# A two-layer encoder trunk: block products in another order, probability scaling on ScalarE, memory's keys and values first

## The chip, the cores and the metric

The kernel runs on one core of one Trainium2 chip. The metric is device time in microseconds (us) of one execution, the median of several runs; lower is better. The engines of the core have short names in the profile: PE is TensorE (PEld its weight loads), DVE is VectorE, ACT is ScalarE, POOL is GpSimd, and SP is SyncE, which here only issues DMAs. All matrix products are on PE; DVE, ACT and POOL do what lies between them.

## What is computed

The input is x of 512 tokens by 1024, and a memory of 256 tokens by 1024. Two layers follow each other. Each has one wide projection of the normalised x, a token mixer, a cross attention to the memory (4 heads), a SiLU gate and an output projection that is added to x:

```python
h = rmsnorm(x, norm_g[i]);  mem_h = rmsnorm(mem, mem_norm_g[i])
proj = jnp.einsum('bsd,de->bse', h, w_in_a[j])     # layer B: w_in_b
o_mix = mixer_dilated(qkv, ...)                     # layer B: mixer_axial_gqa
o_mem = memory_attention(q_mem, mem_h, w_mem_kv[i], ...)
y = jnp.concatenate([o_mix, o_mem], axis=-1) * jax.nn.silu(gate)
x = x + jnp.einsum('bse,ed->bsd', y, w_out[i])
```

Layer A mixes with three dilated windows per head (8 heads), layer B with grouped-query attention over all 512 tokens (8 query heads). Queries and keys are normalised per head and, in the mixers, rotated; each attention is a softmax over scores.

## The kernel before

**Numbers in two parts.** Every float32 operand of the large products is split into a high part (a cast to fp32r) and a low part (the operand minus the high part). A product is three matmuls: high by high, high by low, low by high (`mm3`, L163 to L165). For weights the high part is `wh`, cast on ACT (`hi`, L282), and the low part `wo`, subtracted on DVE (`lo`, L292); for activations the two parts are made the same way in `split` (L157 on ACT, L160 on DVE).

**Seven block products.** A projection to 512 columns (a chunk) is done as a 2x2 block product with seven products in place of eight. `ORDER` (L173) names the weight blocks in the order of use: the stored blocks "11", "21", "12", "22" and the sums T1, T2, T3, T4 of them. `PRODUCTS` (L347) names the activation block, the PSUM bank (0 or 1) and whether the bank starts afresh: A-blocks "11", "12", "22" and the sums S1, S2, S3, S4. `s_chunk` (L349) runs through them; behind each product an entry of `after` copies the bank to SBUF (`keep`, L357 on ACT) or adds it to what was kept (`add`, L367 on DVE). In the kernel before, the quadrant "22" is a subtraction between two copies in SBUF (L361, DVE), 33 times. The finished quadrant goes on to an `ev` of the chunk (norm, rotation, gate).

**Weights.** The class `Weights` walks through `PLAN`, a list of chunk kinds. It loads tiles of 128x1024 (512 KB) by SP's queue as long as fewer than `KEEP[kind]` tiles are alive. The sum T1 is made on DVE (L251) for chunks ahead of `T1_DMA`, and by an accumulating DMA from POOL's queue for the others; T2, T3 and T4 are accumulating DMAs from POOL's queue always (L256, L261, L266). `KEEP`, `LEAD` and `RING` set how early each is issued.

**The order of the work.** Each engine has its own in-order queue, and the Python code writes them in one pass. `Driver` counts slots, one for each weight tile's products. Side tasks are generators: `urgent` ones (evacuation, norms, preparing the next operand) are stepped when due, `bulk` ones (the attentions) once a slot, with some half-slot steps where `HALF` says so (every third one in two of layer B's gate chunks). A `yield n` puts the next step n slots later, so numbers such as `PD`, `EO`, `Y` and `YB` are waiting times in slots.

**The run through.** Layer A: x is normalised and its rows are transposed into the blocks of H (`put_h`, L461), the first chunk (one set of values, `v0`) starts, and the memory's norm (`mem_norm`) and its keys and values (`mem_kv`, 8 groups of 12 matmuls) come behind it. Then follow the memory's queries, the 8 head chunks with `attn_a` in the background, the three gate chunks (m, a, b), and the output projection. For the latter the gated rows `yf` of the first two gate chunks are the right operand: `prep_y` forms their sums by eight 128x512 subtractions and additions on POOL (L778), then splits each (L759 on ACT, L760 on DVE), while the third gate chunk runs. Then the rest of the projection (`out_rest`), memory's keys and values of layer B, its chunks with `attn_b` (32 steps of a 128-query block) in the background, again three gate chunks with `prep_y`, and the output projection. The rotation table of layer B is made on POOL (L1197, four of 128x512).

**Softmax.** In each attention the reciprocal of the row sum is taken and the probabilities are scaled on DVE: `p` in `attn_a` (L1083, 64 pieces), `pm` in `mem_attn` (L645, 32), `pb` in `attn_b` (L1310, 32). PE transposes the scaled tile next (L1096, L654, L1319). `pipeline` sets the stages of one step: score 0, exponential 1, reciprocal and scale 2, transpose 3, product with the values 4.

## Time and profile before

| what | value |
|---|---|
| time, median of 3 runs (lowest, highest) | 991.82 us (990.87, 992.66) |
| span of the profiled execution | 989.9 us |
| runs above that span | lowest 1.0 us, median 1.9 us |
| mean granted TensorE clock | 0.991 |
| busy: PE, DVE, ACT, POOL | 951.5, 830.3, 644.3, 360.9 us |
| matmuls in the trace | 5724 |
| moved by DMA | 206.13 MB, mean 208 GB/s |

No own time of the profiled execution is listed beside its span: the span goes from the first to the last instruction of the program, and what a run has beyond it is the 1.0 to 1.9 us of the table.

How to read it: PE's busy time is a sum in which neighbouring matmuls overlap, so it is not PE at its peak. But where PE's row is short of the length of a stretch, PE waited. The view of waits lists for each engine what ended each idle time.

### The profile page before, as it was taken

How to read it: one execution, taken by the hardware profiler on the slowest of the kernel's cores; microseconds unless marked ns; L12 is line 12 of the kernel's file. 1: busy time of each engine (PE TensorE's matmuls, PEld its weight loads, DVE VectorE, ACT ScalarE, POOL GpSimd, SP SyncE). 2: the span in 40 equal slices, each digit the busy share in tenths (PEclk: the TensorE clock that was granted, in tenths of full speed). 3: DMA queues.
4: the chain of work that ended last, by engine and by line, in shares of the span. 5: the costliest groups of instructions: out<-in, count | busy, mean ns of one | idle time of the engine just before them, and what ended most of it. 6: DMA issues, size and time to landing. Idle time of an engine off the chain costs nothing.

```text
span 989.9 us, 16669 instructions
## 1 busy us (share of the span) xinstructions
PE 951.5 (96%) x5724; PEld 837.7 (85%) x5724; DVE 830.3 (84%) x1471; ACT 644.3 (65%) x1623; POOL 360.9 (36%) x486
## 2 busy tenths in 40 slices
PE   6999999999999999999999979998999999996998
PEld 4789888888888888888899967887999999985886
DVE  6897788879797979797888998878789998889974
ACT  5656678677777777777775745555677766564750
POOL 2232424565555555555542170124632330115000
PEclk9999999999999999999999989999999999997999
DMA  8989946968777777777769785679685877674532
GB/s 335 309 292 346 225 104 174 295 137 240 182 223 184 221 190 216 189 216 169 237 163 291 173 247 151 254 256 318 173 195 125 241 177 211 179 198 117 160 128 85
DMA packets 86966, 206.13 MB, mean 208 GB/s; under 512 B 25057, under 2 KB 35809, under 8 KB 86882
## 3 DMA queue, kind: packets, MB, share of 16 engines
q1 hardware_dynamic: 70034, 146.28, 42.7%
q0 software_dynamic: 15552, 56.63, 30.3%
q10 hardware_dynamic: 1296, 2.16, 0.6%
q8 instruction: 45, 0.74, 0.3%
q14 instruction: 39, 0.32, 0.1%
HBM read 157.79 MB, written 12.65 MB: 172 GB/s over the span
## 4 chain that ended last, share of the span: by engine, by line
PE 70%; DVE 17%; DMA 7%; issue 3%; ACT 1%; POOL 1%; SPq 1%; DVEq 0%; ACTq 0%; POOLq 0%
PE pj L163 18%; PE pj L165 18%; PE pj L164 18%; DVE wo L292 4%; DMA wl<-in_wall_dram 3%; PE qT L531 2%; DMA og<-od 1%; DVE pb L1310 1%; PE sa L1015 1%; PE pt L1096 1%; DVE sn L367 1%; PE oo L1117 1%; PE sa L1011 1%; PE ptb L1319 1%; PE xT L461 1%
## 5 line engine op out<-in xcount | busy, mean ns | idle before, releaser
L292 DVE TENSOR_TENSOR wo<-wl,wh 128x1024 fp32r<-128x1024 f32 x255 | 315.4, 1243 | 10.1 <-ACT wh L282 9.7
L282 ACT CAST wh<-wl 128x1024 fp32r<-128x1024 f32 x255 | 269.7, 1059 | 73.7 <-PE pj L165 41.2
L163 PE MATMUL pj<-wh,hS 128*128 128x512 f32 (+1 forms) x448 | 164.5, 367 | 0.1
L164 PE MATMUL pj<-wo,hS 128*128 128x512 f32 (+1 forms) x448 | 158.1, 353 | 2.1 <-DVE wo L292 2.0
L165 PE MATMUL pj<-wh,hS 128*128 128x512 f32 (+1 forms) x448 | 158.1, 353 | 0.0
L163 PE MATMUL pj<-wh,h 128*128 128x512 f32 (+1 forms) x336 | 123.2, 367 | 0.8 <-ACT h L157 0.8
L164 PE MATMUL pj<-wo,h 128*128 128x512 f32 (+1 forms) x336 | 118.8, 353 | 1.9 <-DVE wo L292 1.9
L165 PE MATMUL pj<-wh,h 128*128 128x512 f32 (+1 forms) x336 | 118.9, 354 | 0.0
L410 POOL TENSOR_TENSOR rstd<-mse,half 128x4 f32<-128x4 f32 (+2 forms) x98 | 102.0, 1040 | 8.2
L164 PEld LDWEIGHTS pj<-wo,hS 128*128 128x128 f32 x448 | 85.0, 190 | 13.0 <-DVE wo L292 3.2
L165 PEld LDWEIGHTS pj<-wh,hS 128*128 128x128 f32 x448 | 84.7, 189 | 12.2
L163 PEld LDWEIGHTS pj<-wh,hS 128*128 128x128 f32 x448 | 84.8, 189 | 10.2 <-ACT sn L357 0.3
L409 POOL TENSOR_SCALAR mse<-hss 128x4 f32<-128x4 f32 (+1 forms) x86 | 45.3, 526 | 110.5 <-ACT junk L519 103.5
L357 ACT COPY sn<-pj 128x512 f32<-128x512 f32 x132 | 73.5, 590 | 16.5 <-PE pj L165 16.1
L959 POOL TENSOR_TENSOR ta<-sn,tabs 128x128 f32<-128x128 f32 (+1 forms) x64 | 37.0, 580 | 121.1 <-DVE sn L524 81.7
L519 ACT ACTIVATE junk<-sn 128x128 f32<-128x128 f32 x264 | 78.9, 307 | 0.2 <-DVE sn L361 0.2
L164 PEld LDWEIGHTS pj<-wo,h 128*128 128x128 f32 x336 | 64.0, 191 | 9.5 <-DVE wo L292 2.2
L165 PEld LDWEIGHTS pj<-wh,h 128*128 128x128 f32 x336 | 63.7, 190 | 9.2 <-DVE h L160 0.2
L367 DVE TENSOR_TENSOR sn<-pj,sn 128x512 f32<-128x512 f32 x99 | 67.4, 683 | 4.6 <-PE pj L165 4.4
L163 PEld LDWEIGHTS pj<-wh,h 128*128 128x128 f32 x336 | 63.9, 190 | 8.4 <-ACT h L157 1.2
L266 POOL DMA_DIRECT2D wl<-wl x33 | 29.4, 898 | 103.7 <-DVE wo L292 52.3
L163 PE MATMUL pj<-hS,wh 128*128 128x256 f32 x192 | 55.9, 291 | 0.0
(226 smaller groups left out, 2487.1 us busy)
## 6 DMA issues: line engine op xcount, KB each, us to landing
wl<-in_wall_dram SPq DMA_DIRECT2D x222, 512.0 KB, 6.9
wl<-wl POOLq DMA_DIRECT2D x66, 512.0 KB, 5.9
wl<-in_wall_dram POOLq DMA_DIRECT2D x42, 512.0 KB, 8.4
od<-o SPq DMA_DIRECT2D x12, 256.0 KB, 5.0
og<-od SPq DMA_DIRECT2D x12, 256.0 KB, 6.0
odb<-o SPq DMA_DIRECT2D x12, 256.0 KB, 4.0
og<-odb SPq DMA_DIRECT2D x12, 256.0 KB, 3.8
x<-in_x_dram SPq DMA_DIRECT2D x4, 512.0 KB, 5.7
```

The lines of the kernel that those rows point to most:

```text
L163: T.matmul(o, lh, rh, start=start, stop=False, skip_group_check=True)
L164: T.matmul(o, lh, rl, start=False, stop=False, skip_group_check=True)
L165: T.matmul(o, ll, rh, start=False, stop=stop, skip_group_check=True)
L266: G.dma_start(self.tile[key], self.tile[c, "T2", x], accum_op=ALU.add)
L282: A.copy(wh, self.tile[self.items[i]])
L292: V.tensor_tensor(wo, self.tile[key], wh.bitcast(F32), ALU.subtract)
L357: A.copy(t, b)
L367: V.tensor_tensor(t, b, t, ALU.subtract if q == "12" else ALU.add)
L409: G.tensor_scalar(e, ss, EPS, None, ALU.add)
L410: G.tensor_tensor(r, e, half[:, 0:n], ALU.pow)
L519: A.activation(jk, p[:, j * 128:(j + 1) * 128], AF.Square, scale=QS, accum_out=ss[:, j:j + 1])
L959: G.tensor_tensor(ta[:, 0:n], xn[:, 0:n, 0:32], ropeA[:, 0, b, s0:s0 + n], ALU.mult)
```

## The change

1. **Products.** `ORDER`, `LOADS` and `PRODUCTS` are reordered: 11, 12, S2, S1, S3, S4, 22 on the activation side, with weights 11, 21, T2, T1, T3, 22, T4. It is the same seven pairs. The quadrant "22" is now a subtraction of the bank from a kept copy, so that the subtraction between two copies goes. In the output projections (`direct`) the last quadrant is added to x straight from PSUM.
2. **Scaling.** The scaling of `p`, `pm` and `pb` goes to ACT (a Copy with a scale per row). The factor 0.5 of the gate moves into the coefficients, or into the values. In the two `pipeline`s the reciprocal becomes a stage of its own, and the last stage is 5 instead of 4.
3. **Start.** Two memory tiles are loaded first. Memory's keys and values of layer A are the first chunks of the plan, and x is normalised and transposed by the side task `prep` behind them.
4. **prep_y and the rotation table.** The eight sums of each `prep_y` and layer B's table are made on DVE.
5. **Numbers.** Waiting times of side tasks, `KEEP`, and `T1_DMA` (17 to 14: the T1 sums of the last gate chunk and of layer A's output projection go from DVE to accumulating DMAs).

```diff
-XW, BOTH = (1, 2, 0, 5), False
-BULK, ACTIVE, MEM_AT, SET_AT, WARM, MEM_B, PREP_Y, ACC_AT, PREP_B, HALF, SET_B = 2, 2, 5, 15, 1, 12, 1, 4, 1, {"a": 3, "b": 3, "o": 0}, 11
+XW = (0, 0, 0, 5)
+HALF = {'a': 2, 'b': 3, 'o': 0}
+PB = {'mem': (1, 2, 3, 4, 5), 'b': (1, 2, 3, 4, 5)}
-EO = 1, 2, 1, 1, 1
+EO = (1, 3, 1, 2, 1)
-T1_DMA = 17
+T1_DMA = 14
...
-    ORDER = ("21", "11", "T1", "T2", "22", "T3", "T4")
+    ORDER = ("11", "21", "T2", "T1", "T3", "22", "T4")
...
-    PRODUCTS = (("12", 0, True), ("11", 1, True), ("S1", 0, True), ("S2", 1, False), ("S4", 0, False), ("S3", 1, False), ("22", 0, True))
+    PRODUCTS = (("11", 1, True), ("12", 0, True), ("S2", 1, False), ("S1", 0, True), ("S3", 1, False), ("S4", 0, False), ("22", 1, False))
...
-            if name == "s3":
-                c = snap["s5", u]
-                V.tensor_tensor(c, c, t, ALU.subtract)
-                yield 1
-                yield from ev("22", u, c)
...
+            if q == "22":
+                V.tensor_tensor(t, t, b, ALU.subtract)
+            else:
+                V.tensor_tensor(t, b, t, ALU.subtract if q == "12" else ALU.add)
...
+        def recip(i):
+            V.reciprocal(pr[i][1], pr[i][1])
+
         def scale(i):
-            _, den, pp = pr[i]
-            rd = sm(1, "rdb")
-            V.reciprocal(rd, den)
-            V.tensor_scalar(pp, pp, rd, 0.5, ALU.mult, ALU.mult)
+            _, rd, pp = pr[i]
+            A.activation(pp, pp, AF.Copy, scale=rd)
...
-                V.tensor_scalar(prob[o][:, b, c0:c1], prob[o][:, b, c0:c1], c[:, o, b:b + 1], 0.5, ALU.mult, ALU.mult)
+                if SCALE_A:
+                    A.activation(prob[o][:, b, c0:c1], prob[o][:, b, c0:c1], AF.Copy, scale=c[:, o, b:b + 1])
...
-            for o, p, q, op in ((s1, a21, a22, ALU.subtract), (s2_, s1, a11, ALU.subtract),
-                                (a12, a12, s2_, ALU.add), (a21, a11, a21, ALU.subtract)):
+            for o, p, q, op in ((s1, a21, a22, ALU.subtract), (s2_, s1, a11, ALU.subtract)):
                 for j in range(2):
-                    G.tensor_tensor(o[j], p[j], q[j], op)
+                    V.tensor_tensor(o[j], p[j], q[j], op)
...
-    nc.sync.dma_start(row0, norm_g[0:1, :])
+    nc.sync.dma_start(row0, mem_norm_g[0:1, :])
+    mt = [m4(name="m") for _ in range(2)]
+    for b in range(2):
+        nc.sync.dma_start(mt[b], mem[b * 128:(b + 1) * 128])
+        W.dma(MW[b])
+    row_load("x0", norm_g[0:1, :])
...
-    drv.spawn(mem_norm(0), MEM_AT)
-    s_chunk(512, H, ev_v0, pre=second)
-    km, vm = mem_kv(0, Ms[0])
+    km, vm = mem_kv(0, M, pre)
+    s_chunk(512, H, ev_v0)
...
-                G.tensor_tensor(ropeB[:, qk, cs_].rearrange("p b (h e) -> p b h e", h=2),
+                for b in range(4):
+                    V.tensor_tensor(ropeB[:, qk, cs_, b].rearrange("p (h e) -> p h e", h=2),
...
```

How instructions move, at three places. First `prep_y` of layer A, while the third gate chunk runs. On POOL before, the sums `ys` and `yf` stand in one piece, with the weight sums (`wl`) ahead and behind:

```order
L266 DMA wl<-wl 128x1024
L256 DMA wl<-wl 128x1024 x2
L778 TENSOR_TENSOR ys<-yf 128x512 x2
L778 TENSOR_TENSOR ys<-ys,yf 128x512 x2
L778 TENSOR_TENSOR yf<-yf,ys 128x512 x2
L778 TENSOR_TENSOR yf<-yf 128x512 x2
L266 DMA wl<-wl 128x1024 x2
L261 DMA wl<-in_wall_dram 128x1024 x2
```

On DVE now, at the same place (L811 and L817 are the sums, L794 the split of `yS`, L316 the weights' low parts, L757 and L769 the gate):

```order
L316 TENSOR_TENSOR wo<-wl,wh 128x1024
L811 TENSOR_TENSOR ys<-yf 128x512 x2
L811 TENSOR_TENSOR ys<-ys,yf 128x512 x2
L757 SCALAR_TENSOR_TENSOR th<-th,sn 128x512
L389 TENSOR_TENSOR sn<-sn,pj 128x512
L316 TENSOR_TENSOR wo<-wl,wh 128x1024
L794 TENSOR_TENSOR yS_7046<-ys,yS_7046 128x512 x2
L769 TENSOR_TENSOR th<-th,og 128x512
L391 TENSOR_TENSOR sn<-pj,sn 128x512
L316 TENSOR_TENSOR wo<-wl,wh 128x1024
L794 TENSOR_TENSOR yS_7084<-ys,yS_7084 128x512 x2
L817 TENSOR_TENSOR yf<-yf 128x512 x2
```

The eight have left POOL; four stand together on DVE, and the others between the splits.

Second, ACT in layer B's output projection, with `attn_b` in the background, before (L1304 is the exponential, L1323 the high part of the transposed tile, L282 the weights' high part, L759 the split of `y`):

```order
L282 CAST wh<-wl 128x1024
L759 CAST y_11409<-yf 128x512 x2
L738 CAST y<-sn 128x2x256
L1304 ACTIVATE pb,denb<-sb,nmb 128x512
L1323 CAST pbT<-ptb 128x4x128
```

The same stretch now (L306 are the weights, L793 and L772 the splits, L1361 the exponential, L1381 the transposed tile):

```order
L306 CAST wh<-wl 128x1024
L793 CAST y_11207<-yf 128x512 x2
L1368 ACTIVATE pb<-pb,denb 128x512
L1361 ACTIVATE pb,denb<-sb,nmb 128x512
L1381 CAST pbT<-ptb 128x4x128
L306 CAST wh<-wl 128x1024
```

The scaling, L1368, stands between the weights' cast and the exponential of a later step.

Third, PE in the first chunk of x, where a sum S is first used, before (`xs` are the sums of x's rows that PE transposes, `h_175` the block 11, `hS_282` the block S1):

```order
L165 MATMUL pj<-wh,h_175 128x512
L461 MATMUL xT<-ident,xs_235 128x128 x4
L163 MATMUL pj<-wh,hS_282 128x512
L164 MATMUL pj<-wo,hS_282 128x512
L165 MATMUL pj<-wh,hS_282 128x512
```

And now (`h_404` is the block 12, `hS_584` the block S2):

```order
L186 MATMUL pj<-wh,h_404 128x512
L493 MATMUL xT<-ident,xs_529 128x128 x4
L493 MATMUL xT<-ident,xs_560 128x128 x4
L184 MATMUL pj<-wh,hS_584 128x512
L185 MATMUL pj<-wo,hS_584 128x512
L186 MATMUL pj<-wh,hS_584 128x512
```

Both halves of the operand are now transposed directly ahead of their product; before it was only the second half.

More of the change, by code (lines that the diff above doesn't have):

```diff
@@ L180, in __init__ @@
             self.users = {}
-            d = g = 0
+            first, d, g = {}, 0, 0
+            for c in (2, 0, 1, *range(3, len(PLAN))):
+                first[c] = d
+                d += 4 if PLAN[c] in ("T2", "T2b", "W1", "W1b") else 2 if PLAN[c] == "O1" else 8
+            assert d == wall.shape[0], (d, wall.shape)
             for c, kind in enumerate(PLAN):
-                base = len(self.items)
+                base, d = len(self.items), first[c]
                 if kind in GROUPS:
@@ L326, in trunk_kernel, with chunk @@
     W = Weights()
-    def chunk(units, nb, group, evac):
+    def chunk(units, nb, group, evac, pre=None):
         ps = [None] * nb
@@ L480, in group @@
                 mm3(p, sels[b](act, 0, kk), sels[b](act, 1, kk), w[k][0], w[k][1], kk == 0, kk == 7)
-        chunk(2, len(sels), group, evac)
+        chunk(2, len(sels), group, evac, pre)
     part = {}
@@ L677, in out_ @@
                 put(h, os)
-        yield from pipeline(8, (0, score, 0), (4, pv, 0), (3, turn, 0), (2, scale, 0), (1, exps, 0),
-                            (0, top, 1), (3, hi, 1), (3, lo, 1), (4, out_, 1), step=step)
+        e, r, c, t, v = PB["mem"]
+        yield from pipeline(8, (0, score, 0), (v, pv, 0), (t, turn, 0), (r, recip, 0), (c, scale, 0), (e, exps, 0),
+                            (0, top, 1), (t, hi, 1), (t, lo, 1), (v, out_, 1), step=step)
     def out_rest(ys, acc, done, evac):
@@ L783, in prep_y @@
             yield 1
-            for k, src in (("S4", a12), ("S3", a21), ("22", a22)):
-                put(k, src)
-                yield 1
+            put("S1", s1)
+            for j in range(2):
+                V.tensor_tensor(a21[j], a11[j], a21[j], ALU.subtract)
+            yield 1
+            put("S3", a21)
+            for j in range(2):
+                V.tensor_tensor(a12[j], a12[j], s2_[j], ALU.add)
+            yield 1
+            put("S4", a12)
+            yield 1
+            put("22", a22)
+            yield 1
         return gate, prep_y, YW, ys
@@ L808, in out_proj @@
         drv.spawn(load(), ACC_AT)
-        s_chunk(512, YW, ev, half=half)
+        s_chunk(512, YW, ev, half=half, direct=True)
         out_rest(ys, acc, done, evac)
     xv = x.rearrange("(p c) d -> c p d", c=4)
-    xt = [m4(name="x") for _ in range(4)]
     rows = {}
@@ L819, in trunk_kernel @@
     row0 = m4(name="row0")[0:1, :]
-    nc.sync.dma_start(row0, norm_g[0:1, :])
-    rows["x0"] = halves(row0)
+    nc.sync.dma_start(row0, mem_norm_g[0:1, :])
+    rows["m0"] = halves(row0)
+    mt = [m4(name="m") for _ in range(2)]
[3 more added lines that the diff above has]
+    row_load("x0", norm_g[0:1, :])
+    xt = [m4(name="x") for _ in range(4)]
     for c, n in enumerate(XW):
@@ L833, in trunk_kernel @@
     xb = [halves(t) for t in xt]
-    nst = {}
+    mb = [halves(t) for t in mt]
     def prep():
+        row = rows["x0"]
+        r = [norm_1(xb[0])]
+        yield PD[0]
+        for c in range(2):
+            r.append(norm_1(xb[c + 1]))
+            norm_2(xb[c], r[c], row)
+            yield PD[1]
+            put_h(H, "11", c, xb[c][0])
+            yield PD[1]
+        for c in range(2):
+            put_h(H, "12", c, xb[c][1])
+            if not c:
+                r.append(norm_1(xb[3]))
+            yield PD[2]
         s1, sums = [], []
         for c in range(2):
-            norm_2(xb[2 + c], nst[2 + c], first)
+            norm_2(xb[2 + c], r[2 + c], row)
+            yield PD[2]
             s1.append(sum_h(xb[2 + c]))
         for c in range(2):
-            yield PD[1 + c]
             sums_h(H, xb[c], xb[2 + c], c, s1[c], sums)
-        yield PD[3]
-        yield from rest_h(H, sums)
+            yield PD[3]
+        yield from rest_h(H, sums, PD[4])
     def setup():
```

161 lines of the change are left out of this document (93 added, 68 removed).

## The prediction

> **What bounds the kernel now.** I read the page first, then stretches of the span, then the waits of PE, then the timeline at the two longest of them. The page's busy times, and its 40 slices for PE and the granted clock:
>
> ```profile
> PE 951.5 (96%) x5724; PEld 837.7 (85%) x5724; DVE 830.3 (84%) x1471; ACT 644.3 (65%) x1623; POOL 360.9 (36%) x486
> PE   6999999999999999999999979998999999996998
> PEclk9999999999999999999999989999999999997999
> ```
>
> PE bounds the kernel nearly everywhere, and the change leaves its matmuls as they are. What can be won is PE's idle time: 989.9 - 951.5 = 38.4 us, and what a slow clock behind a long pause adds. Two dents in PE's row, at slices 24 and 37, have a dent in the clock too. The view of stretches gives each stage (columns: PE, PEld, DVE, ACT, POOL busy us, clock, DMA share, GB/s):
>
> ```profile
> 22.40:45.00 22.60, 18.64 (x97) 14.80 (x96) 19.09 (x25) 11.99 (x17) 4.62 (x5) 1.00 1.05 300
> 45.00:545.00 500.00, 499.92 (x2799) 432.64 (x2798) 412.92 (x839) 354.79 (x1009) 241.35 (x352) 1.00 0.78 217
> 569.00:594.00 25.00, 18.56 (x97) 15.62 (x96) 23.92 (x24) 11.25 (x18) 18.53 (x12) 0.86 0.88 245
> 668.00:696.00 28.00, 24.54 (x166) 21.73 (x166) 25.00 (x36) 16.40 (x38) 10.79 (x8) 1.00 1.05 320
> 770.00:820.00 50.00, 49.14 (x390) 46.95 (x389) 49.40 (x85) 34.55 (x90) 15.88 (x18) 1.00 0.81 205
> 891.00:904.00 13.00, 5.17 (x33) 4.53 (x32) 12.96 (x7) 3.97 (x9) 10.70 (x9) 0.75 0.42 101
> ```
>
> From 45 to 545 us PE waits 0.08 us in 500: layer A's head chunks have nothing to give, so the subtractions and scalings that leave DVE there win nothing. The rest sits in short stretches where DVE is full. The waits of PE say for what (us in total, times, longest):
>
> ```profile
> PE ptb L1319 <- DVE pb L1310: 7.8, 1, 7.8
> PE pj L163 <- DVE sn L367: 7.3, 2, 6.3
> PE pj L164 <- DVE wo L292: 3.9, 3, 1.9
> PE xT L461 <- DVE xs L496: 3.5, 2, 1.9
> PE ob L164 <- DVE pbT L1328: 2.8, 2, 1.8
> ...
> PE pt L1096 <- DVE p L1083: 1.3, 3, 0.5
> ```
>
> All of these end on DVE. The first two are single waits, each beside POOL's eight sums of `prep_y`. The late one in the timeline (start, us; idle before in brackets):
>
> ```profile
> 891.63 2.87 POOL L778 TENSOR_TENSOR ys<-yf 128x512 f32<-128x512 f32 x2
> 899.02 2.76 POOL L778 TENSOR_TENSOR yf<-yf 128x512 f32<-128x512 f32 x2
> 891.79 10.28 DVE L1310 TENSOR_SCALAR pb<-pb,rdb 128x512 f32<-128x512 f32 x1
> 902.22 1.09 PE L1319 MATMUL ptb<-ident,pb 128*128 128x128 f32 x4 [7.83 <-DVE pb L1310]
> 902.96 0.78 PE L163 MATMUL pj<-wh,y 128*128 128x512 f32 x1
> 907.72 0.39 PE L165 MATMUL pj<-wh,y 128*128 128x512 f32 x1
> 907.95 0.39 PE L163 MATMUL sb<-kbT,qb 128*128 128x512 f32 x1
> ```
>
> One scaling on DVE lasts 10.28 us: it starts 0.16 us behind POOL's first sum and ends as the last one does. PE stands 7.83 us. Then eleven matmuls take 907.72 - 902.96 = 4.76 us, where the next step is 0.23: 4.76 - 11 x 0.23 = 2.2 us more, for the clock. The mid one, with DVE's groups from 572 to 587 us in the middle:
>
> ```profile
> 571.91 3.84 POOL L778 TENSOR_TENSOR ys<-yf 128x512 f32<-128x512 f32 x2 [4.56 <-DVE yf L732]
> 583.56 3.37 POOL L778 TENSOR_TENSOR yf<-yf 128x512 f32<-128x512 f32 x2
> L760 DVE TENSOR_TENSOR yS<-ys,yS 128x512 fp32r<-128x512 f32 x2 | 3.5, 1764 | 0.0
> L292 DVE TENSOR_TENSOR wo<-wl,wh 128x1024 fp32r<-128x1024 f32 x3 | 6.3, 2112 | 0.0
> 589.09 0.80 PE L163 MATMUL pj<-wh,y 128*128 128x512 f32 x1 [6.33 <-DVE sn L367]
> 593.80 0.39 PE L165 MATMUL pj<-wh,y 128*128 128x512 f32 x1
> ```
>
> **The change part by part.** The durations that I use, DVE's and then ACT's (busy us and mean ns of one behind the bar):
>
> ```profile
> L361 DVE TENSOR_TENSOR sn<-sn 128x512 f32<-128x512 f32 x33 | 23.3, 733 | 0.0
> L732 DVE TENSOR_TENSOR yf<-sn,og 128x512 f32<-128x512 f32 x16 | 10.9, 684 | 2.9 <-DMA og<-od 2.7 <-PE sb L165 0.2
> L251 DVE TENSOR_TENSOR wl<-wl 128x1024 f32<-128x1024 f32 x24 | 29.4, 1226 | 0.0
> L1310 DVE TENSOR_SCALAR pb<-pb,rdb 128x512 f32<-128x512 f32 x32 | 25.4, 793 | 1.1
> L1083 DVE TENSOR_SCALAR p<-p,c 128x256 f32<-128x256 f32 x48 | 14.0, 349 | 0.0
> L954 ACT COPY v<-sn 128x256 f32<-128x256 f32 x32 | 12.7, 398 | 0.0
> L993 ACT ACTIVATE p<-p,st 128x256 f32<-128x256 f32 x48 | 24.1, 506 | 2.2 <-DVE st L1021 2.2
> L1304 ACT ACTIVATE pb<-sb,nmb 128x512 f32<-128x512 f32 x32 | 22.2, 693 | 19.7 <-DVE nmb L1300 15.8 <-PE ptb L1319 2.3 <-DMA odb<-o 1.3
> ```
>
> *prep_y, mid.* POOL's sums run from 571.91 to 586.93, 15.0 us. In that time DVE's 128x512 steps take 1764 ns instead of 684 and the 128x1024 ones 2112 instead of 1226, so about half of DVE's time, 7.5 us, is lost. Gone are 6.33 us of wait and, by 593.80 - 589.09 = 4.71 us for eleven steps, 2.2 us of slow clock: 8.5. What comes in: eight sums on DVE, 8 x 0.684 = 5.5 us. DVE is then 7.5 - 5.5 = 2.0 us earlier by this alone. But the T1 sums that leave DVE (three, 3 x 1.226 = 3.7) and the subtractions between copies (one in each of two gate chunks, two in the output projection: 4 x 0.733 = 2.9, of which not all come in time) lie here too: up to 8.6 us against the 6.3 that it was late. I let 1.5 us stay: **-7.0**, bounds 0 and -8.5.
>
> *prep_y, late.* The blocked scaling gives DVE 10.28 - 0.49 = 9.8 us (0.49 is the mean of the other 31: 25.4 - 10.28 = 15.1 us by 31), less 5.5 for the sums: 4.3 us earlier. PE stood 7.83, so 3.5 would be left, were it not that each step of `attn_b` also loses its 0.49 on DVE, one every 5 us. Gone at most 7.83 + 2.2 = 10.0, and a rest under 3.5 us seems too short for the clock to fall: the waits of up to 1.9 us in 668 to 696 stand beside a clock of 1.00. I let 1.5 stay: **-8.5**, bounds -3 and -10.
>
> *Scaling on ACT.* 48 pieces of 128x256, 16 of 128x192 and 32 of 128x256 (`pm`) between the copy's 398 and the exponential's 506 ns, say 0.45 (it reads a scale per row, as the exponential reads its bias), and 32 of 128x512 by 0.693: 96 x 0.45 + 32 x 0.693 = 65 us. ACT goes from 644 to 709 of some 970 us. In the fullest stretch, 770 to 820, it has 34.55 of 50; nine steps add 6.2: 40.8. So its cover is 9 us in 50. Each stage is a slot behind the one that it waits for, and the weights' casts queue behind the scalings. I cost it at nothing to PE from 45 to 545, and at +1 in layer B; without that cover it is the slower rival below.
> The Trainium skill speaks against this edit: "ScalarE: Activation LUTs", section Rules for kernel authors, wants a `mul` on VectorE, not on ScalarE. By its formula (section What ACT_TABLE_LOAD costs, 280 ns and 0.833 a column with one operand per row) a piece would be 493 or 706 ns, an estimate of 70 us in place of 65; the row of the exponential, 693, is near it. The sum would not change by that.
>
> *Other waits on DVE behind 545 us.* They are 3.5 (`xs`), 2.8 (`pbT`), 1.3 (`p`) and 7.3 - 6.3 = 1.0: 8.6. The row sums `xs` of layer B move behind the start of its first chunk and get more slots (`EO`), POOL's rotation table leaves that stretch (10.79 us of POOL busy there), and `pb` and `p` no longer are DVE's. Some will come back elsewhere: **-5**, bounds 0 and -8.6.
>
> *The start.* Memory first: the queue is now memory, weight, memory, two weights, gain row, and the first x tile seventh. Before, the first and third loads were x tiles:
>
> ```profile
> 4.88 0.63 ACT L448 ACTIVATE sq<-x 128x512 f32<-128x512 f32 x1 [2.65 <-DMA x<-in_x_dram]
> 7.81 0.63 ACT L448 ACTIVATE sq<-x 128x512 f32<-128x512 f32 x1 [0.28 <-DMA x<-in_x_dram]
> 9.66 0.80 PE L163 MATMUL pj<-wh,h 128*128 128x512 f32 x1 [0.80 <-ACT h L157]
> ```
>
> (7.81 - 4.88) / 2 = 1.47 us a tile, so the seventh is there at 4.88 + 6 x 1.47 = 13.7. ACT's square of it stands ahead of the second memory tile's casts, but the first group of 12 matmuls at the slow step of 0.43 lasts from 9.66 to 14.8 and hides that. The 3.9 us that PE waits for `wo` in 22 to 45 us (DMA share 1.05) should go, for the memory's weights need no sums and x's first chunk gets 20 us more of loading. In return all of x's norms, splits and sums fall on DVE in the memory's groups and two products: by the code some 14 steps of 1.226 and 28 of 0.684 from the second pair of weights to S2, 36 us, beside 120 matmuls of 0.23 and the transposes, 31 on PE; and both halves of S2 are transposed directly ahead of their product. So up to 5 us come back at S2. Net **0**, bounds -4 and +5.
>
> The sum: -7.0 - 8.5 + 1 - 5 + 0 = -19.5, on the span 989.9 - 19.5 = 970.4. The median of the runs is 1.9 above the span, so 972.3 us; 0.2% (2 us) is about what a measurement of this kernel can tell from no change.
>
> **The rivals.**
> 1. *DVE is late again at the same places.* The sums are now in its own queue, ahead of `wo` and the evacuation that PE waits for. For it: DVE has no idle in 891 to 904. Against: 4 to 10 us are freed there. Half of the two stalls and none of the smaller waits: 989.9 - 9 + 1.9 = 982.8.
> 2. *More than that.* No rest at either stall (-18.5), all 8.6 and the 3.9 at the start: 989.9 - 31 + 1.9 = 960.8. Against: each place must come out at its bound.
> 3. *Not POOL.* The 10.28 us are a wait that only coincides with POOL; then only the smaller terms hold: about 989.9 - 5 + 1.9 = 986.8. Against: two places, and DVE is slowed in both just as long as POOL runs.
> 4. *ACT's queue becomes the bound, slower than before.* A scaling waits for its reciprocal, and the weights' cast and exponential behind it wait as well. ACT has 15.4 us idle in 770 to 820; it decides from the point where over 9 us of that cannot be filled because they are waits in a queue. Then each scaling of layer B adds to the time: 32 x 0.693 + 16 x 0.45 = 29 us: 970.4 + 29 + 1.9 = 1001.3. The rule of the skill above would have this. Against: a slot between all stages.
>
> **How the numbers follow.** Forecast 0.60 (its own range, by the bounds of the start and of the two stalls, 964 to 981), DVE late again 0.17, more 0.10, not POOL 0.05, ACT 0.08. The range 961 to 985 holds the first two and nearly all of the third. Faster: 0.60 + 0.17 + 0.10 + 0.05 = 0.92, less 0.01 for a sum that ends within 0.2%: 0.91; same 0.01; slower 0.08.
>
> **What would show it.** Right: no DVE scaling of several us, no clock under 0.95 behind 50 us, DVE's 128x512 steps near 0.684 in both `prep_y`, PE's idle (38.4 now) under 26 us in all. Rival 1: PE's longest waits are on `yS`, `wo` or `sn` while the sums run on DVE. Rival 4: PE waits for ACT's `wh` or `pbT` in layer B, and ACT is full there. At the start, a wait of PE on DVE's split of S2 near 50 us would show the price that I set against the `wo` waits. A span above 984 would make the forecast wrong.

## The result, and the profile after

The changed kernel takes 979.34 us (median of four runs, 974.98 to 980.94), the kernel before 992.24 on the same chip. The ratio of the runs, as it is on record for every kernel below, is 0.9855, 95% interval 0.9833 to 0.9877 (the two medians alone would give 0.9870). It is faster by 1.5%, 7.0 us above the time predicted and inside the range. The profiled execution took 978.73 us with a span of 977.0; before, the span was 989.9. The page of the changed kernel, the three rows that answer to those of before:

```profile
PE 951.3 (97%) x5724; PEld 837.8 (86%) x5724; DVE 760.1 (78%) x1339; ACT 697.1 (71%) x1747; POOL 325.9 (33%) x469
PE   7899999999999999999999998998999999999998
PEclk9999999999999999999999999998999999999999
```

PE's busy time is the same (951.5 before), so its idle time fell from 38.4 to 977.0 - 951.3 = 25.7 us. The dents at slices 24 and 37 are gone; one is left in the clock, at slice 28. DVE has 70 us less to do, ACT 53 more. The stretches (PE, PEld, DVE, ACT, POOL busy us, clock, DMA share, GB/s), with the two `prep_y` where they lie now:

```profile
22.40:45.00 22.60, 19.92 (x92) 16.19 (x92) 18.48 (x24) 15.32 (x40) 14.51 (x17) 0.92 1.01 376
45.00:545.00 500.00, 497.45 (x2775) 429.23 (x2774) 384.63 (x758) 376.33 (x1054) 231.91 (x344) 1.00 0.80 211
565.00:605.00 40.00, 36.29 (x219) 31.18 (x218) 35.04 (x56) 27.47 (x46) 5.23 (x6) 1.00 1.06 293
668.00:696.00 28.00, 25.09 (x161) 22.75 (x160) 23.18 (x32) 13.60 (x19) 5.73 (x7) 0.88 0.96 300
770.00:820.00 50.00, 50.00 (x402) 48.81 (x401) 45.44 (x77) 41.03 (x101) 13.52 (x16) 1.00 0.84 216
870.00:905.00 35.00, 33.28 (x231) 30.36 (x231) 32.52 (x55) 29.23 (x58) 5.85 (x7) 1.00 0.89 223
```

The reader should see that PE fills 770 to 820 us completely with ACT at 41.03 of 50 (the prediction had 40.8), and that 45 to 545, where PE waited 0.08 us before, now lacks 2.6 us: the start reaches into it. What PE waits for now (us in total, times, longest):

```profile
PE qT L562 <- DVE xn L555: 5.5, 2, 2.9
PE pj L185 <- DVE wo L316: 4.3, 5, 1.3
...
PE ob L185 <- DVE pbT L1386: 2.5, 2, 1.3
PE pj L184 <- ACT act L178: 2.1, 1, 2.1
...
PE pj L184 <- DVE vm L630: 1.2, 1, 1.2
```

The waits of 7.8 and 6.3 us are gone, no wait is over 2.9. DVE's sums and splits in the mid `prep_y` (columns: busy us, mean ns of one):

```profile
L794 DVE TENSOR_TENSOR yS<-ys,yS 128x512 fp32r<-128x512 f32 x4 | 2.6, 680 | 0.0
L811 DVE TENSOR_TENSOR ys<-yf 128x512 f32<-128x512 f32 x2 | 1.3, 684 | 0.0
```

The split of `yS` took 1764 ns beside POOL's sums; now it takes 680, and a sum on DVE 684.

To compare all runs place by place I use one measure. For each matmul I take the time from its start to the next one's start and subtract the median of that time over the matmuls of its line and shape in the same run. Summed over a stretch, that is what PE lost there, waits and slow clock together. The stretches are the start (0 to 130 us), the mid `prep_y` (545 to 630), the rows between the layers (655 to 700), layer B's chunks (700 to 870), the late `prep_y` (870 to 925) and the end.

| kernel | median us | ratio to before, 95% interval | start | mid | rows | layer B | late | end |
|---|---|---|---|---|---|---|---|---|
| before | 992.2 | 1 | 11.7 | 12.4 | 4.1 | 2.2 | 12.7 | 2.3 |
| after | 979.3 | 0.9855 [0.9833, 0.9877] | 15.6 | 5.0 | 5.9 | 0.5 | 4.1 | 0.8 |
| e1 after, sums on POOL | 980.0 | 0.9875 [0.9854, 0.9895] | 15.0 | 8.7 | 4.2 | 0.5 | 3.2 | 1.5 |
| e2 before, sums on DVE | 984.1 | 0.9917 [0.9898, 0.9937] | 13.0 | 8.1 | 5.6 | 2.6 | 6.4 | 3.2 |
| e3 after, scaling on DVE | 981.3 | 0.9883 [0.9858, 0.9907] | 17.3 | 6.7 | 4.7 | 0.3 | 4.3 | 1.4 |
| e4 before, scaling on ACT | 992.5 | 1.0004 [0.9991, 1.0017] | 13.2 | 8.5 | 5.0 | 3.5 | 11.3 | 5.3 |
| e5 after, sums on POOL in one piece | 982.2 | 0.9892 [0.9873, 0.9910] | 15.9 | 6.0 | 2.7 | 0.4 | 7.6 | 2.7 |
| e6 before, POOL's sums spread | 993.5 | 1.0013 [1.0001, 1.0025] | 12.4 | 12.8 | 6.9 | 2.6 | 12.6 | 1.7 |
| e7 after, old start | 981.9 | 0.9894 [0.9877, 0.9911] | 20.7 | 4.6 | 4.4 | 0.4 | 3.5 | 1.1 |
| e8 after, T1 by DMA | 977.1 | 0.9844 [0.9822, 0.9865] | 18.3 | 5.2 | 3.1 | 0.4 | 2.5 | 1.2 |
| e9 before, new order alone | 1004.2 | 1.0110 [1.0097, 1.0124] | 21.5 | 9.8 | 7.4 | 13.7 | 4.3 | 1.4 |
| e10 after, neither relief of DVE | 984.1 | 0.9904 [0.9889, 0.9919] | 16.0 | 7.2 | 4.3 | 0.4 | 8.0 | 2.6 |
| e11 before, both reliefs | 986.1 | 0.9929 [0.9917, 0.9942] | 13.4 | 5.5 | 4.9 | 3.2 | 9.2 | 4.1 |
| e12 = e8 and EO | 977.4 | 0.9844 [0.9824, 0.9866] | 17.5 | 5.1 | 4.3 | 0.4 | 4.5 | 1.1 |

Each row is one profiled execution. How far such a number can be trusted is seen where several kernels have the same code at a place: in the rows between the layers six kernels (after, e1, e3, e5, e7, e8) give 2.7 to 5.9, at the start five (after, e1, e3, e5, e10) 15.0 to 17.3. Differences under 3 us at one place are not read as an effect below. For the rows the traces show where the scatter comes from: PE waits there for the same normalization for 2.57 to 2.91 us in each of the six, and behind it the granted clock of the next 4 us is 1.00 in e5 and e8 but 0.60 in e1 and 0.63 in e7.

By this table, one execution of each kernel, the changed kernel gained 7.4 us at the mid `prep_y`, 8.6 at the late one, 1.7 in layer B and 1.5 at the end, and lost 3.9 at the start and 1.8 in the rows. That is 13.7 with 0.2 from 130 to 545 us; the medians of the steps themselves sum to 0.7 us more, and the spans differ by 12.9.

### The profile page after: what moved, and what is told of

Its sections match the earlier page's. It is cut to its first block, busy times and chain, and to the rows that moved or that the text cites. A ratio compares the mean times of both kernels' runs of the same rounds, so it can differ in the third digit from the quotient of the medians.

```text
span 977.0 us, 16605 instructions
## 1 busy us (share of the span) xinstructions
PE 951.3 (97%) x5724; PEld 837.8 (86%) x5724; DVE 760.1 (78%) x1339; ACT 697.1 (71%) x1747; POOL 325.9 (33%) x469
## 4 chain that ended last, share of the span: by engine, by line
PE 83%; DMA 8%; DVE 6%; issue 2%; ACT 1%; SPq 0%; DVEq 0%; ACTq 0%
PE pj L186 22%; PE pj L184 21%; PE pj L185 21%; DMA wl<-in_wall_dram 3%; PE qT L562 2%; DVE wo L316 2%; DMA og<-od 2%; PE sa L1067 1%; PE oo L1172 1%; PE pt L1151 1%; PE sa L1063 1%; DMA og<-odb 1%; PE ptb L1377 1%; DMA x1d<-acc 1%; PE xT L493 1%
## 5 line engine op out<-in xcount | busy, mean ns | idle before, releaser
L316 DVE TENSOR_TENSOR wo<-wl,wh 128x1024 fp32r<-128x1024 f32 x255 | 312.5, 1229 | 11.8 <-ACT wh L306 11.5
L306 ACT CAST wh<-wl 128x1024 fp32r<-128x1024 f32 x255 | 270.1, 1060 | 70.4 <-PE pj L186 41.7
L442 POOL TENSOR_TENSOR rstd<-mse,half 128x4 f32<-128x4 f32 (+2 forms) x98 | 109.2, 1114 | 8.2
L186 PEld LDWEIGHTS pj<-wh,hS 128*128 128x128 f32 x448 | 84.7, 189 | 12.8 <-DVE hS L181 0.4
L185 PEld LDWEIGHTS pj<-wo,hS 128*128 128x128 f32 x448 | 85.0, 190 | 11.3 <-DVE wo L316 1.5
L441 POOL TENSOR_SCALAR mse<-hss 128x4 f32<-128x4 f32 (+1 forms) x86 | 34.4, 400 | 164.6 <-ACT junk L550 161.0
L1011 POOL TENSOR_TENSOR ta<-sn,tabs 128x128 f32<-128x128 f32 (+1 forms) x64 | 39.2, 612 | 123.1 <-DVE sn L555 112.3
L383 ACT COPY sn<-pj 128x512 f32<-128x512 f32 x99 | 55.3, 595 | 11.1 <-PE pj L186 10.8
L186 PE MATMUL pj<-hS,wo 128*128 128x256 f32 x192 | 54.3, 283 | 0.0
```

What stands on the lines that cost most here:

```text
L185: T.matmul(o, lh, rl, start=False, stop=False, skip_group_check=True)
L186: T.matmul(o, ll, rh, start=False, stop=stop, skip_group_check=True)
L306: A.copy(wh, self.tile[self.items[i]])
L316: V.tensor_tensor(wo, self.tile[key], wh.bitcast(F32), ALU.subtract)
L383: A.copy(t, b)
L441: G.tensor_scalar(e, ss, EPS, None, ALU.add)
```

## The experiments

**e1, the sums back to POOL.** In the changed kernel, `prep_y` alone:

```diff
-                    V.tensor_tensor(o[j], p[j], q[j], op)
+                    G.tensor_tensor(o[j], p[j], q[j], op)
...
-                V.tensor_tensor(a21[j], a11[j], a21[j], ALU.subtract)
+                G.tensor_tensor(a21[j], a11[j], a21[j], ALU.subtract)
...
-                V.tensor_tensor(a12[j], a12[j], s2_[j], ALU.add)
+                G.tensor_tensor(a12[j], a12[j], s2_[j], ALU.add)
```

> The changed kernel (979.3 us) with one part undone: the eight sums of each prep_y are issued on POOL again; order, scalings and start stay as changed. Theory A, that the two stalls beside POOL's sums made the gain and taking the sums off POOL ended them: both stalls come back, the mid one with 6 to 8 us, the late one with 3 to 10 (the DVE scaling that was blocked there is on ACT now, so DVE may only be stretched): 988 to 996 us, DVE 128x512 steps of 1.5 us or more beside the sums, and a clock under 0.95 in one of the two places. Theory B, that the order of the products and the scalings on ACT freed DVE and so made the gain, wherever the sums run: 977 to 983 us.

980.0 us: by its time theory B. By its places theory A, which is the prediction's own cause, is half right. POOL's sums stretch DVE again, up to 3.08 us for a 128x1024 step of 1.21 and 4.16 us for a 128x512 split of 0.68. At the mid place the stall is back, and the place loses 3.7 us more than in the changed kernel; at the late one PE isn't late, and nothing is lost. DVE and PE of e1 at the mid place:

```profile
581.69 3.43 DVE L769 TENSOR_TENSOR th<-th,og 128x512 f32<-128x512 f32 x1
586.91 0.79 PE L185 MATMUL pj<-wo,y 128*128 128x512 f32 x1 [5.44 <-DVE wo L316]
```

The granted clock is 0.63 from 585 to 590 us and 0.69 from 590 to 595. That the time hardly shows it is the sum of smaller differences elsewhere (1.7 us less in the rows), none of which is an effect by itself.

**e2, the sums to DVE in the kernel before.**

```diff
-                    G.tensor_tensor(o[j], p[j], q[j], op)
+                    V.tensor_tensor(o[j], p[j], q[j], op)
```

> The kernel before (992.2 us) with one part of the change alone: prep_y's eight sums go from POOL to DVE, in the old place and order. Theory A: both stalls go but for a rest, 975 to 981 us, as much as the whole change or more, since the start (which I read as 4 us worse behind the change) stays as it was. Theory B: DVE is as full as before and has 5.5 us of sums more in each place, so PE still waits there: 987 to 993 us.

984.1 us, above what theory A gave and below theory B. By its ratio the sums alone are worth 0.0083 x 992 = 8.2 us: 4.3 at the mid place, 6.3 at the late one, some of it lost again elsewhere. So they are enough to end the long stalls, but 8.1 and 6.4 us stay.

**e3, the scalings back to DVE** in the changed kernel (`p`, `pm`, `pb`):

```diff
-SCALE_A = True
+SCALE_A = False
...
-            A.activation(pp, pp, AF.Copy, scale=rd)
+            V.tensor_scalar(pp, pp, rd, None, ALU.mult)
```

> The changed kernel (979.3 us) with the scalings of p, pm and pb on DVE again, in the same slots. Theory A: layer A's head chunks have nothing to lose and layer B little, 979 to 983 us. Theory B: DVE is full again where the gain was made, 985 to 992 us. If the scalings are a burden on ACT that PE pays (the slower rival of the prediction in a small size), it becomes faster: 974 to 978.

981.3 us: theory A, with an interval that overlaps that of the changed kernel. No place differs by over 1.7 us. That the scaling on ACT is worth anything here is not shown; 2 us lie between the medians.

**e4, the scalings of `p` and `pb` to ACT in the kernel before** (the factor 0.5 goes into the coefficients and into `vb`; the stages stay, so a scaling stands in the slot of its reciprocal):

```diff
-                V.tensor_scalar(prob[o][:, b, c0:c1], prob[o][:, b, c0:c1], c[:, o, b:b + 1], 0.5, ALU.mult, ALU.mult)
+                A.activation(prob[o][:, b, c0:c1], prob[o][:, b, c0:c1], AF.Copy, scale=c[:, o, b:b + 1])
...
-            V.tensor_scalar(pp, pp, rd, 0.5, ALU.mult, ALU.mult)
+            A.activation(pp, pp, AF.Copy, scale=rd)
```

> The kernel before (992.2 us) with one part of the change alone: the scalings of p and pb go to ACT (those of pm stay on DVE), POOL keeps its sums. Theory A in its narrow form, that the late stall was one DVE scaling blocked for 10.28 us while POOL ran: the late stall shrinks to the stretch of ordinary DVE steps, 984 to 989 us, the mid stall (6.3 and 2.2 us) stays. Theory A in its wide form, that any DVE work beside POOL's sums loses the same time: 989 to 993 us. Theory B: 976 to 984 us.

992.5 us, no change: the wide form of theory A. The timeline of e4 at the late place, POOL, DVE, ACT and PE (start, us; idle before in brackets):

```profile
891.54 2.88 POOL L778 TENSOR_TENSOR ys<-yf 128x512 f32<-128x512 f32 x2
899.02 2.77 POOL L778 TENSOR_TENSOR yf<-yf 128x512 f32<-128x512 f32 x2
892.99 0.69 DVE L1329 TENSOR_TENSOR pbT<-ptb,pbT 128x512 fp32r<-128x512 f32 x1 [0.73 <-ACT pbT L1324]
893.60 9.28 DVE L292 TENSOR_TENSOR wo<-wl,wh 128x1024 fp32r<-128x1024 f32 x1
903.04 0.72 ACT L1311 ACTIVATE pb<-pb,denb 128x512 f32<-128x512 f32 x1 [7.18 <-DVE denb L1307]
904.29 0.58 PE L163 MATMUL ob<-pbT,vb 128*128 128x256 f32 x1 [6.10 <-ACT pbT L1324]
```

There is no scaling on DVE any more, and the hold falls on the next step, a subtraction of two SBUF operands: 9.28 us where it takes 1.21, until 1.1 us behind the end of POOL's series, which had begun 2.1 us earlier. The step ahead of it, which reads PSUM, takes its usual 0.69 beside POOL. The reciprocal is queued behind the held step, ACT waits 7.18 us for it and PE 6.10 for ACT. So the hold is no property of the scaling, as the prediction's row might suggest. The mid place loses 8.5 us in place of 12.4, but the wait of PE for `sn` is still there with 5.74 us.

**e5, the sums on POOL in one piece** in the changed kernel:

```diff
-            for o, p, q, op in ((s1, a21, a22, ALU.subtract), (s2_, s1, a11, ALU.subtract)):
+            for o, p, q, op in ((s1, a21, a22, ALU.subtract), (s2_, s1, a11, ALU.subtract),
+                                (a21, a11, a21, ALU.subtract), (a12, a12, s2_, ALU.add)):
                 for j in range(2):
-                    V.tensor_tensor(o[j], p[j], q[j], op)
+                    G.tensor_tensor(o[j], p[j], q[j], op)
             yield 1
...
+            for k, src in (("S2", s2_), ("S1", s1), ("S3", a21), ("S4", a12), ("22", a22)):
+                put(k, src)
+                yield 1
```

> Undoing the sums' engine alone cost the changed kernel nothing (980.0 against 979.3 us), and in that run POOL's eight sums stood in three groups, each ahead of the split that needs it, where DVE's longest step beside them was 3.5 us. Theory C, that what held DVE for 10 us in the kernel before was that the eight sums ran back to back: the changed kernel with the eight sums on POOL and back to back again, ahead of the first split, gets a DVE step of 8 to 10 us in the late prep_y, a PE wait of 4 to 8 us behind it and a slow clock, 985 to 991 us. Theory D, that the new order of the products gives PE more slack there, whatever the sums do: 978 to 982 us.

982.2 us: theory D's range but for 0.2 us, and no hold as in theory C. The late loss rises from 4.1 to 7.6, but not beside the sums: there no DVE step is over 1.78 us and PE waits 1.26. POOL and DVE of e5 during the sums, POOL behind them, and then DVE and PE 25 us behind them:

```profile
878.94 3.53 POOL L812 TENSOR_TENSOR ys<-ys,yf 128x512 f32<-128x512 f32 x2
885.40 3.99 POOL L812 TENSOR_TENSOR yf<-yf,ys 128x512 f32<-128x512 f32 x2
880.00 1.32 DVE L316 TENSOR_TENSOR wo<-wl,wh 128x1024 fp32r<-128x1024 f32 x1
881.25 1.77 DVE L757 SCALAR_TENSOR_TENSOR th<-th,sn 128x512 f32<-128x512 f32 x1
886.45 3.49 DVE L794 TENSOR_TENSOR yS<-ys,yS 128x512 fp32r<-128x512 f32 x2
889.34 1.80 POOL L280 DMA_DIRECT2D wl<-wl  x2
890.47 2.46 POOL L285 DMA_DIRECT2D wl<-in_wall_dram  x2
...
914.45 0.69 DVE L769 TENSOR_TENSOR th<-th,og 128x512 f32<-128x512 f32 x1 [4.23 <-DMA og<-odb]
922.22 0.58 PE L185 MATMUL ob<-pbT,vb 128*128 128x256 f32 x1 [3.72 <-DVE pbT L1376]
```

The two engines take turns: POOL's pairs take up to 3.99 us where the first took 2.53, DVE's step 1.77 instead of 0.68. In the kernel before that was so at the mid place, but not at the late one. What this run lost at the late place is a wait of another kind: DVE stands 4.23 us for the transfer of the mixer's output that the gate multiplies, and PE later 3.72 for the steps queued behind it.

The queues of the trace lead this wait back to the sums all the same. Four weight DMAs that POOL issues stand behind the sums and start together, at 889.34 to 891.00 us; in the changed kernel they start at 879.85, 883.71, 892.38 and 893.56. The weight sums `wl<-wl` of 870 to 930 us then take 10.3 us (median) from issue to landing, in place of 5.4, and SP's queue, which must see the mixer's output stored before it loads it, waits up to 7.4 us for the store in place of 2.8. That the bunched DMAs slow the store is read from these times; it wasn't tried alone.

**e6, POOL's sums in three groups** (four, two, two) in the kernel before:

```diff
-                                (a12, a12, s2_, ALU.add), (a21, a11, a21, ALU.subtract)):
+            for o, p, q, op in ((s1, a21, a22, ALU.subtract), (s2_, s1, a11, ALU.subtract)):
...
+            put("S2", s2_)
+            for j in range(2):
+                G.tensor_tensor(a12[j], a12[j], s2_[j], ALU.add)
+            yield 1
+            put("S4", a12)
+            for j in range(2):
+                G.tensor_tensor(a21[j], a11[j], a21[j], ALU.subtract)
```

> The kernel before (992 us) with its sums left on POOL, but in three groups (four, two, two), each ahead of the split that needs it. Theory C: no DVE step over 5.5 us beside them, the late loss of 12.7 us falls to 3 to 7, the mid one of 12.4 to 8 to 11, 981 to 987 us, about as much as moving the sums to DVE gave there (984.1). Theory D: the old order of the products keeps both stalls, 989 to 993 us.

993.5 us: theory C fails. At the late place the hold is cut into 5.43, 3.56 and 3.52 us, one for each group, and the loss stays at 12.6. At the mid one a 128x512 split is held 7.17 us, beside two groups that follow each other, and PE waits 7.84 us. In the old order spreading doesn't help; in the new one (e1) the late place doesn't lose.

**e7, the old start** in the changed kernel (cut; the mirror of the diff shown, with "11" ahead of "12"):

```diff
-PLAN = ["T2"] * 2 + ["W2", "W1", "W2s"] + ["W2" if c.isdigit() else "W1" for c in A_ORDER[1:]] + ["W2"] + ["O1"] * 2 + ["T2b"] * 2 + ["W1b"] * 7 + ["W2b"] + ["O1"] * 2
+PLAN = ["W2"] + ["T2"] * 2 + ["W1", "W2s"] + ["W2" if c.isdigit() else "W1" for c in A_ORDER[1:]] + ["W2"] + ["O1"] * 2 + ["T2b"] * 2 + ["W1b"] * 7 + ["W2b"] + ["O1"] * 2
...
-    km, vm = mem_kv(0, M, pre)
-    s_chunk(512, H, ev_v0)
+    drv.spawn(mem_norm(0), MEM_AT)
+    s_chunk(512, H, ev_v0, pre=second)
+    km, vm = mem_kv(0, Ms[0])
```

> The changed kernel (979.3 us) with the start of the kernel before: x's rows first, then the first x chunk in the new order of its products, the memory's keys and values behind it. By PE's loss up to 130 us (15.6 us behind the change, 11.7 before) memory first costs 4 us: 974 to 977 us. If the later stages need memory first (weights loaded further ahead, norms out of the way), 979 to 984. As the prediction had it (a start worth 0): 978 to 981.

981.9 us. My reading that memory first costs 4 us was wrong: against the old start in the new order it saves 5 us at its place (20.7 to 15.6), of which 2.6 are left in the medians, with intervals that touch. The time lies in the second range, but the loss is at the start and not in the later stages that this range was for. ACT, DVE and PE of e7:

```profile
32.92 1.04 ACT L307 CAST wh<-wl 128x1024 fp32r<-128x1024 f32 x1 [11.81 <-DMA wl<-wl]
34.00 1.23 DVE L317 TENSOR_TENSOR wo<-wl,wh 128x1024 fp32r<-128x1024 f32 x1 [5.47 <-ACT wh L307]
35.97 1.08 PE L494 MATMUL xT<-ident,xs 128*128 128x128 f32 x4 [5.52 <-DVE xs L536]
```

`wl<-wl` is the sum T2, an accumulating DMA that adds T1. In the old order T1 was third and T2 fourth; in the new one T2 is third, and it still needs T1 first. ACT stands 11.81 us for it, and DVE and PE behind ACT. So behind the old start it is the new order that costs some 9 us (20.7 against 11.7), and memory first gives over half of it back.

**e8, T1 of the first x chunk by DMA** in the changed kernel:

```diff
+    def t1_dma(c):
+        return c == 2 or c >= T1_DMA
...
-                if k == "T1" and c >= T1_DMA:
+                if k == "T1" and t1_dma(c):
```

> The changed kernel (979.3 us) with one edit: the T1 sum of the first x chunk's weights is made by an accumulating DMA from the weights in DRAM instead of two 128x1024 additions on DVE, one of which stood idle 1.93 us for a transfer at 31.7 to 33.6 us, ahead of the normalization that PE then waited 2.7 us for. Theory: that wait goes, 976 to 978.5 us. Rival: the transfer lands later than the two operands did and PE waits as long for it, 979 to 982 us.

977.1 us, in the theory's range, but it can't be told from the changed kernel (the intervals overlap), and it is not there for the reason given: the start lost 18.3 us instead of 15.6, with a wait of PE for ACT's split of S2:

```profile
34.12 0.63 PE L565 MATMUL qT<-ident,xn 128*128 128x128 f32 x4 [1.71 <-DVE xn L558]
59.60 0.80 PE L184 MATMUL pj<-wh,hS 128*128 128x512 f32 x1 [2.49 <-ACT hS L178]
```

The wait for the normalization shrank from 2.56 to 1.71 us, and 2.25 more came at S2. What it has less of lies where the code is the same: 2.8 us in the rows, where a wait of 2.91 us left the clock of the next 4 us at 1.00, while in the changed kernel it stood at 0.50 behind a wait of the same length. That is luck.

**e9, the new order alone** in the kernel before (orders, `s_chunk`, the order of the sums and splits; old start, old steps, POOL's sums in one piece, scaling on DVE):

```diff
-    ORDER = ("21", "11", "T1", "T2", "22", "T3", "T4")
+    ORDER = ("11", "21", "T2", "T1", "T3", "22", "T4")
...
-    PRODUCTS = (("12", 0, True), ("11", 1, True), ("S1", 0, True), ("S2", 1, False), ("S4", 0, False), ("S3", 1, False), ("22", 0, True))
+    PRODUCTS = (("11", 1, True), ("12", 0, True), ("S2", 1, False), ("S1", 0, True), ("S3", 1, False), ("S4", 0, False), ("22", 1, False))
```

> The kernel before (992 us) with the new order of the products alone: x first as before, prep_y's eight sums back to back on POOL (in the order that the new products need), scalings on DVE, old step numbers. The changed kernel with the old start lost 20.7 us of PE up to 130 us, where the kernel before lost 11.7, so the new order behind the old start should cost 9 us there. Theory D, that the order also gives the slack at the two prep_y: their losses (12.4 mid, 12.7 late) fall to 5 to 8 each, 986 to 994 us. Theory F, that the order gives nothing there: 998 to 1003 us.

1004.2 us, slower by 1.1%. Its time is next to theory F, 1.2 us above that range; by its places neither theory holds: the late place lost only 4.3, with POOL's sums and DVE's scalings both there, the mid one 9.8. What neither theory had are 13.7 us in layer B. POOL, ACT and PE there:

```profile
708.30 7.92 POOL L1198 TENSOR_TENSOR tabs<-tbraw,grB 128x512 f32<-128x512 f32 x4 [12.60 <-DVE grB L1195]
717.63 0.93 POOL L256 DMA_DIRECT2D wl<-wl  x1
722.30 1.05 ACT L282 CAST wh<-wl 128x1024 fp32r<-128x1024 f32 x1 [8.90 <-DMA wl<-wl]
728.22 0.58 PE L163 MATMUL pj<-wh,hS 128*128 128x256 f32 x1 [3.95 <-ACT sn L357]
```

It is T2 again: its DMA is issued by POOL behind the rotation table (708.30 to 716.22), ACT's cast waits 8.90 us for it, the copies behind the cast are late, and PE stands 3.95; with the slow clock behind it that is 6.6 of the 13.7 us (720 to 740). A second such cast waits 6.52 us for `wl<-wl` up to 809 us, and PE 2.51 behind it. In the kernel before the table stood at the same place, but T2 was needed one product later. That the new order needs the table off POOL, as the changed kernel has it, is read from this queue; it wasn't tried alone.

**e10, neither relief of DVE** in the changed kernel: the edits of e3 and e5 together.

```diff
-SCALE_A = True
+SCALE_A = False
...
-                    V.tensor_tensor(o[j], p[j], q[j], op)
+                    G.tensor_tensor(o[j], p[j], q[j], op)
```

> The changed kernel (979.3 us) with both reliefs of DVE undone together: the eight sums on POOL back to back, and the scalings on DVE. Alone, the first gave 982.2 us and the second 981.3. Theory D, that order, start and slots carry the gain: the two prices add, 982 to 986 us. Theory F, that either relief covers for the other: a DVE scaling is held beside the sums again, 988 to 993 us with a late loss over 10 us.

984.1 us: theory D. All the rest of the change (order, start, steps, the T1 sums and the table) gives 0.0096 x 992 = 9.5 us with the sums on POOL in one piece and all scalings on DVE. No DVE step is held over 2.33 us, and the late loss of 8.0 has a wait of 3.65 in it that follows stands of DVE for `og`, 2.21 and 2.73 us, as in e5.

**e11, both reliefs without the rest**: the edits of e2 and e4 in the kernel before.

```diff
-                    G.tensor_tensor(o[j], p[j], q[j], op)
+                    V.tensor_tensor(o[j], p[j], q[j], op)
...
-            V.tensor_scalar(pp, pp, rd, 0.5, ALU.mult, ALU.mult)
+            A.activation(pp, pp, AF.Copy, scale=rd)
```

> The kernel before (992 us) with the sums on DVE and the scalings of p and pb on ACT, in the old order of the products and with the old start. Alone they gave 984.1 and 992.5 us. If the scalings are worth nothing in any company: 982 to 986 us. If they make the room on DVE that the sums then use: 978 to 981 us, and the reordered products and the new start would be worth nothing beside them.

986.1 us, no better than the sums alone (984.1). In the old steps no use of the scalings is seen beside them: at 6.0 us in three waits, ACT's `pbT` is among PE's largest. DVE, ACT and PE of e11:

```profile
892.34 1.29 DVE L778 TENSOR_TENSOR ys<-yf 128x512 f32<-128x512 f32 x2
895.96 1.28 DVE L778 TENSOR_TENSOR yf<-yf 128x512 f32<-128x512 f32 x2
897.41 0.72 ACT L1311 ACTIVATE pb<-pb,denb 128x512 f32<-128x512 f32 x1 [3.93 <-DVE denb L1307]
898.65 0.38 PE L163 MATMUL ob<-pbT,vb 128*128 128x256 f32 x1 [2.85 <-ACT pbT L1324]
```

The eight sums stand in one piece in DVE's queue, 892.34 to 897.24, ahead of the reciprocal; ACT's scaling waits 3.93 us for it, and PE 2.85.

**e12, e8 with another EO.**

```diff
-EO = (1, 3, 1, 2, 1)
+EO = (3, 1, 1, 2, 1)
```

> The changed kernel with the T1 sum of the first x chunk by DMA (977.1 us) and one number more: the second normalization step of the output rows comes two slots later (EO begins with 3, 1 in place of 1, 3). There DVE stands 4.43 us for the store of the same tile at 657.0 to 661.4 us, with the weights' low halves and the keys' normalization, for which PE waits 2.9 us at 669.5, queued behind. Theory: the stand and the wait go, and the slow clock behind it: 972 to 975.5 us. Rival: the splits of layer B's first operands then come too late, 977 to 981 us.

977.4 us, the rival's range: no gain over e8, the theory fails. DVE's stand of 4.43 us for the store is gone, but the keys' normalization is then queued behind another step of the rows:

```profile
672.24 1.40 DVE L490 SCALAR_TENSOR_TENSOR acc<-acc,rstd,row 128x512 f32<-128x512 f32 x2
673.57 0.68 DVE L558 TENSOR_TENSOR xn<-pj,rstd 128x512 f32<-128x512 f32 x1
674.40 1.09 PE L565 MATMUL qT<-ident,xn 128*128 128x128 f32 x4 [2.87 <-DVE xn L558]
```

No version was shown to be faster than the changed kernel; e8 and e12 are below it by 2 us with overlapping intervals.

## Why the prediction was right, and where it was not

- **Both stalls: size right, cause half right.** Predicted -7.0 and -8.5, measured -7.4 and -8.6. At the late place the prediction counted on two things: the sums leaving POOL, which by its working are worth 4.3 us and the slow clock of 2.2, and the scalings leaving DVE, which should bring the rest down to 1.5. The first came: e2 has the sums alone and gains 6.3 there; 6.4 stay, of which 12.7 - 10.0 = 2.7 were outside the stall. The second is the step that failed: with the scalings back on DVE the changed kernel loses no more there (e3, 4.3 against 4.1), and with `p` and `pb` on ACT beside the sums in the old steps 9.2 stay (e11). At the mid place the sums alone gain 4.3, where the working gave them 2.0 and gave 6.6 to the T1 sums and the subtractions; what these are worth wasn't tried. In the place of the failed step stands the rest of the change: without either relief (e10) it gives 9.5 us in the time. So that the sum of the two terms came out within 0.5 us is in part luck.
- **How far the parts add up.** By the ratios the whole change gives 0.0145 x 992 = 14.4 us, e2 8.2 and e10 9.5, together 17.7; e11, which has both reliefs, gives 7.0, and with e10 that is 16.5. With intervals of some 2 us on each, the parts may overlap, but that is not shown. What the sums on POOL cost is smaller in the changed kernel: by the ratios 2.0 (e1) to 3.7 us (e5), neither clear of the noise, against 8.2.
- **What stays open.** What in the new order keeps PE from waiting beside the sums at the late place is not settled, and order, steps, T1 sums and table were not taken apart. e9, e5 and e10 have POOL's eight sums in one piece, but DVE is never held for the whole of them. I can't say from these runs why DVE takes turns with POOL there, and at the mid place before, and is held at the late place before, in e4 and in e6 (there at the mid one too).
- **"Not POOL"** (rival 3) is out: e2 changed nothing but the engine of the sums. In e4, e6 and before the held step of the late place ends 0.3 to 1.1 us behind POOL's series.
- **The start: 0 predicted, +3.9 measured**, inside the bounds given, and with the other kernels of each kind 15.0 to 17.3 against 11.7 to 13.4. The step that failed is that I saw only memory first and its price at S2 (which came to 0.24 us). The order has a price of its own, T2 as the third product: 21.5 us at the start of e9 and 20.7 in e7. Memory first takes back 5 of the 9. What the changed kernel still loses more than before lies elsewhere: 4.3 us from 30 to 40 us, for a wait of 2.56 for the normalization of memory's keys and a clock of 0.57 in the 4 us behind it, and 2.2 from 50 to 60; at 20 to 30 it loses 3.2 less.
- **Other waits: -5 predicted, -1.4 in the two profiles** (rows +1.8, layer B -1.7, end -1.5). The rows scatter by 3.2 us with the same code, so nothing is shown there. The 10.79 us of POOL that the prediction took for the rotation table are not the table, which starts at 696.89, behind that stretch; they are steps of the normalizations, one of them 4.27 us long, and DMA issues. That PE still waits 2.9 us in the rows was wrong in the prediction: the wait for `xs` went, one for `xn` came, in the queue behind the row steps.
- **A rest under 3.5 us "seems too short for the clock to fall"** is wrong. PE of the changed kernel:

```profile
672.42 1.09 PE L562 MATMUL qT<-ident,xn 128*128 128x128 f32 x4 [2.91 <-DVE xn L555]
673.73 0.63 PE L185 MATMUL pj<-wo,act 128*128 128x512 f32 x1
678.00 0.62 PE L186 MATMUL pj<-wh,act 128*128 128x512 f32 x1
```

  Behind a wait of 2.91 us ten steps take 678.00 - 673.73 = 4.27 us, 0.43 each where this step else takes 0.23, and the granted clock of 674 to 678 us is 0.50. At this place the clock of the next 4 us was 0.58 behind 2.64 us (e10), 0.60 behind 2.65 (e1) and 0.63 behind 2.76 (e7), but 1.00 behind 2.57 (e5) and behind 2.91 (e8). So in these runs a wait of 2.6 to 2.9 us may slow the clock or not. The Trainium skill, "TensorE: Matmul & The Clock Gate", section Why this matters for your kernels, asks for no gap over about 3 us. These runs are nearer to that than to my 3.5, and shorter gaps slowed the clock too.
- **Scaling on ACT: the work was sized right** (65 us predicted; `p` 28.0, `pm` 14.6 and `pb` 23.4 are 66.0), the price of +1 is not seen. Rival 4 did not come: PE has no wait on ACT in 770 to 820 us. e4 and e11 fit what spoke against it, a slot between all stages: there the scaling shares a slot with its reciprocal, and where DVE is late with the reciprocal, PE waits for ACT's `pbT`, 9.3 and 6.0 us in all. The rule of the Trainium skill that wants a `mul` on VectorE ("ScalarE: Activation LUTs", Rules for kernel authors) does not decide here: obeying it in e3 gave 981.3 us against 979.3, a difference inside the noise.
- **Signs named beforehand.** Right: no long DVE scaling, DVE's sums and splits at 676 to 688 ns in both `prep_y`, PE's idle at 25.7 (under 26). Wrong: the clock of slice 28. Rival 1's sign is not there: in the mid `prep_y` PE waits for `wo` four times, up to 1.3 us, but from 588 to 602 us, behind the last of the sums (585.5). The time lies between the forecast (972.3) and that rival (982.8), nearer to the latter, and the range holds both; what speaks for the forecast is that both stalls are gone, with the start and the other waits dearer by 3.9 + 3.6 = 7.5 us. The forecast's own range of 964 to 981 doesn't follow from the bounds that it names: all taken at once, those of the start and the two stalls give 965.3 to 989.8.
